# Places of the matmul operands in SBUF, and two MLP rounds written another way, in a one-layer decoder kernel

## The chip, the core and the metric

The kernel runs on one core of one Trainium2 chip. TensorE (PE) multiplies, reading both operands from SBUF and writing to PSUM; VectorE (DVE), ScalarE (ACT) and GpSimd (POOL) do the rest, and SyncE (SP) issues most of the DMAs. The metric is the device time of one execution in microseconds; less is better.

A product on TensorE has a stationary operand of 128x128, brought in by its own instruction (LDWEIGHTS, shown as engine PEld), and a moving operand of 128 rows and up to 512 columns that streams through (MATMUL, engine PE). The profile gives with every stretch the granted clock of TensorE, as a share of full speed.

## What is computed

One layer of a decoder on a sequence of 256 positions of width 2048, in float32:

```python
h = rms_norm(x, norm1_g)
q_a, k_a, v_a, f_a, q_b, k_b, v_b = split(h @ w_in)          # 2048 -> 6 x 1024 + 8
y_a = fox_attention(q_a, k_a, v_a, log_sigmoid(f_a + forget_b))   # 8 heads of 128
y_b = dilated_attention(q_b, k_b, v_b, rel_bias)                  # 8 heads of 128
x = x + concat(rms_norm(y_a, outnorm_a_g), rms_norm(y_b, outnorm_b_g)) @ w_out
h = rms_norm(x, norm2_g)
x = x + square(relu(h @ w_mlp_in)) @ w_mlp_out               # 2048 -> 8192 -> 2048
return rms_norm(x, final_norm_g)
```

## The kernel before

**Split products.** Every large matrix product is made of three: each operand is split into a high part (the value rounded to float32r) and a low part (the rest), and hi x hi, lo x hi and hi x lo are added up in PSUM. Activations are held split, transposed to features x positions: `aT_hi` and `aT_lo` (16 rows of 256 positions on each partition), and `big_hi` and `big_lo`, which serve the attention output (`yT`) first and the hidden layer of the MLP (`hT`) later. A row of 256 float32 is 1024 bytes, so all 16 rows of such a tile begin at the same place in a 256-byte line. An empty tile `ahead` of 8 elements stands before them and shifts that place to element 8 of the line's 64.

**Weights.** They come by DMA from HBM through four buffers `raw` (512 rows x 512 columns each) and are split in steps of 256 rows: ACT copies to `whi` (L178), DVE subtracts and writes `wlo` (L179). Both have four buffers, and each buffer has 64 elements more than it needs, so that a step's data can begin at a chosen place in the line. The places are constants: `LINE, NEAR, HIGH, LOW, GATED = 64, 8, 24, 56, 48`. Where weights are stationary (chunks `q`, `k` and `u`, named in `TURNED`), `whi` begins at element 24 and `wlo` at element 56; where they are the moving operand (`v`, `o`, `d`), both begin at 8; in the one `v` chunk that also holds the forget gates, at 48 and 16, or 56 and 24 for the second row of a step.

**Chunks.** The work is a list of chunks of 512 weight columns: three for each of four head groups (`q`, `v`, `k`), eight for the output projection (`o`), and four MLP rounds (`r` = 0 to 3) of four up chunks (`u`) and four down chunks (`d`). A `u` chunk has 16 feature rows `kt`, and for each 12 products: four blocks of 128 weight columns (stationary) times three terms, with 256 positions moving (`turned_product`, L340). A `d` chunk has for each of 16 `kt` six products: two halves `t` of the positions (stationary) times three terms, with 512 weight columns moving (`product`, L323 to L325). So a `u` half-round has 4 x 16 x 12 = 768 products of 256 columns and a `d` half-round 4 x 16 x 6 = 384 products of 512: 196,608 columns each. The last chunk of all (`last_chunk`) is written in three pieces, the last two with 256 moving columns.

**Order.** The program is written out by hand, engine by engine. Each step's two rows of products are followed by what `at(slot, ...)` hung there: drains of finished accumulators, scores, transposes and values of the attention heads, norms. Weights are split three steps (`LEAD`) ahead of their products and loaded two to three steps ahead of the split. Accumulators have four PSUM banks, two to a chunk.

**Attention scratch.** `scores` writes `neg` (two buffers), which ACT reads for the exponential. `values` squares a head's output into `sqt` (one buffer, L582 and L584), which POOL adds to `sq` (L586).

Of the kernel before, what the change touches and what calls it, by code (L numbers as in the profile page):

```python
# [11 lines left out]
F32 = mybir.dt.float32  # L12
F32R = mybir.dt.float32r
# [6 lines left out]
P = 128  # L20
D_MODEL = 2048
SEQ = 256
TB = SEQ // P
HD = 128
NH = 8
D_GRP = NH * HD
D_FF = 4 * D_MODEL
KT = D_MODEL // P
CW = 512
# [13 lines left out]
LINE, NEAR, HIGH, LOW, GATED = 64, 8, 24, 56, 48  # L43
# [30 lines left out]
def kernel(  # L74
# [18 lines left out]
    nc = tc.nc  # L93
# [5 lines left out]
    lead_in = ctx.enter_context(tc.tile_pool(name="lead_in", bufs=1))  # L99
    one = ctx.enter_context(tc.tile_pool(name="one", bufs=1))  # L100
    two = ctx.enter_context(tc.tile_pool(name="two", bufs=2))
    wraw = ctx.enter_context(tc.tile_pool(name="wraw", bufs=4))
    wsplit = ctx.enter_context(tc.tile_pool(name="wsplit", bufs=LEAD + 1))
    wide = ctx.enter_context(tc.tile_pool(name="wide", bufs=1))
# [6 lines left out]
    chunks = []  # L111
# [25 lines left out]
    raws, splits = {}, {}  # L137
# [15 lines left out]
    def split(i, j0=0, n=2):  # L153
        if i >= len(steps):
            return
        if j0:
            return split_rows(i, j0, n)
        ci, s = steps[i]
        if ci == len(chunks) - 1 and s < 4:
            hi, lo = (a[:, 4 * s:4 * s + 4, :].rearrange("p (k j) s -> p k (j s)", k=2) for a in (aT_hi, aT_lo))  # L160
        else:
            what, cols = chunks[ci][0], chunks[ci][5]
            high, low = (HIGH, LOW) if what in TURNED else (NEAR, NEAR) if cols == CW else (GATED, HIGH - NEAR)
            hi, lo = (
                wsplit.tile([P, 2 * CW + LINE], F32R, name=n)[:, b:b + 2 * cols].rearrange("p (j c) -> p j c", j=2)
                for n, b in (("whi", high), ("wlo", low))
            )
        splits[i] = (hi, lo)
        split_rows(i, j0, n)

    def split_rows(i, j, n):
        ci, s = steps[i]
        hi, lo = (a[:, j:j + n, :] for a in splits[i])
        t = raws[ci, s // 2][:, 2 * (s % 2) + j:2 * (s % 2) + j + n, :chunks[ci][5]]
        cols = t.shape[2]
        step = cols // 2 if i == j == 0 else cols
        for c in range(0, cols, step):
            nc.scalar.activation(hi[:, :, c:c + step], t[:, :, c:c + step], AF.Copy)  # L178
        nc.vector.tensor_tensor(lo, t, hi.bitcast(F32), op=ALU.subtract)  # L179
# [1 line left out]

    xs = one.tile([P, TB, D_MODEL], F32, name="xs")
    grow = one.tile([48, P], F32, name="grow")
    gT = lead_in.tile([P, 96], F32, name="gT")[:, :48]
    ident = one.tile([P, P], F32, name="ident")
    zeros = two.tile([P, CW], F32, name="nat")
    warm = zeros[:, :CW // 2].bitcast(BF16)
# [60 lines left out]
        nc.vector.tensor_copy(gT[:, k0:k1], p[:, k0:k1])  # L248

    wide.tile([P, NEAR], F32, name="ahead")  # L250
    aT_hi = wide.tile([P, KT, SEQ], F32R, name="aT_hi")
    aT_lo = wide.tile([P, KT, SEQ], F32R, name="aT_lo")

    def split_psum(hi, lo, src, scale=None, early=False):

        if early:

            nc.vector.tensor_scalar(hi, src, scale, None, op0=ALU.mult)
            nc.vector.scalar_tensor_tensor(lo, src, scale, hi.bitcast(F32), op0=ALU.mult, op1=ALU.subtract)
        elif scale is None:  # L260
            nc.scalar.activation(hi, src, AF.Copy)  # L261
            nc.vector.tensor_tensor(lo, src, hi.bitcast(F32), op=ALU.subtract)  # L262
        else:
            nc.scalar.activation(hi, src, AF.Copy, scale=scale)
            nc.vector.scalar_tensor_tensor(
                lo, src, scale, hi.bitcast(F32), op0=ALU.mult, op1=ALU.subtract
            )
# [27 lines left out]
    rstd1 = few.tile([P, TB], F32, name="rstd1")  # L295

    def first_squares(t, c):
        unused = yT_hi[:, 2 * (4 * t + c):2 * (4 * t + c) + 2, :].rearrange("p k s -> p (k s)")
        xc = xs[:, t, c * CW:(c + 1) * CW]
        if t == 0:  # L300
            nc.scalar.activation(unused, xc, AF.Square, accum_out=ssq1[:, t, c:c + 1])
        else:
            nc.vector.tensor_tensor_reduce(unused, xc, xc, 1.0, 0.0, ALU.mult, ALU.add, ssq1[:, t, c:c + 1])
# [6 lines left out]
    accs = {}  # L310

    def operands(what, key):
        if what == "o":
            return yT_hi, yT_lo, key[0] * NH
        if what == "d":
            return hT_hi, hT_lo, 0
        return aT_hi, aT_lo, 0

    def product(acc, a, kt, t, w, j, cols, go, end):

        (ah, al, base), (hi, lo) = a, w
        xh, xl = (p[:, base + kt, t * P:(t + 1) * P] for p in (ah, al))
        nc.tensor.matmul(acc, xh, hi[:, j, cols], start=go, stop=False, skip_group_check=True)  # L323
        nc.tensor.matmul(acc, xl, hi[:, j, cols], start=False, stop=False, skip_group_check=True)  # L324
        nc.tensor.matmul(acc, xh, lo[:, j, cols], start=False, stop=end, skip_group_check=True)  # L325

    def turned_product(ci, i, j, kt, kts):


        if kt == 0:  # L330
            accs[ci] = [psum.tile([P, CW], F32, name="acc", bufs=4) for _ in range(2)]
        hi, lo = splits[i]
        terms = ((hi, aT_hi), (hi, aT_lo), (lo, aT_hi))
        order = [(b, n) for b in range(4) for n in range(3)]
        if i == j == 0:
            order.sort(key=lambda bn: bn[1])
        for b, n in order:
            acc = accs[ci][b // 2][:, b % 2 * SEQ:(b % 2 + 1) * SEQ]
            w, a = terms[n]
            nc.tensor.matmul(acc, w[:, j, b * P:(b + 1) * P], a[:, kt, :],  # L340
                             start=kt == 0 and b % 2 == 0 and n == 0, stop=kt == kts - 1 and n == 2,
                             skip_group_check=True)

    def products(i, j):
        ci, s = steps[i]
        what, key, _, _, _, cols, kts = chunks[ci]
        kt = 2 * s + j
        if what in TURNED:
            return turned_product(ci, i, j, kt, kts)
        a = operands(what, key)  # L350
        if cols > CW:
            return gated_products(ci, i, j, kt, kts, a)
        if kt == 0:
            accs[ci] = [psum.tile([P, CW], F32, name="acc", bufs=4) for _ in range(TB)]
        go, end = kt == 0, kt == kts - 1
        for t in range(TB):
            product(accs[ci][t], a, kt, t, splits[i], j, slice(0, CW), go, end)

    def gated_products(ci, i, j, kt, kts, a):

# [87 lines left out]


    qkv = {}  # L450
    yT_hi = wide.tile([P, 2 * NH, SEQ], F32R, name="big_hi")
    yT_lo = wide.tile([P, 2 * NH, SEQ], F32R, name="big_lo")

    def drain_v(g, ci):
# [109 lines left out]
    sq = [one.tile([P, SEQ], F32, name=f"sq{k}") for k in range(2)]  # L564
    seen = [0, 0]

    def values(g, h):
        half, kind = groups[g][3:]
        hd = kind * NH + half * 4 + h
        vh, vl = qkv[g, "v"]  # L570
        p = turned.pop((g, h))
        y = psum.tile([P, 512], F32, name="sc")
        dims = slice(h * P, (h + 1) * P)
        for n, (v, m) in enumerate(((vh, 0), (vh, 1), (vl, 0))):
            nc.tensor.matmul(y[:, :SEQ], v[:, 0, dims], p[:, m, :SEQ], start=n == 0, stop=False,  # L575
                             skip_group_check=True)
        nc.tensor.matmul(y[:, P:3 * P].rearrange("p (n s) -> p n s", n=2), vh[:, 1, dims], p[:, :, SEQ:],  # L577
                         start=False, stop=False, skip_group_check=True)
        nc.tensor.matmul(y[:, P:SEQ], vl[:, 1, dims], p[:, 0, SEQ:], start=False, stop=True, skip_group_check=True)
        first = seen[kind] == 0  # L580
        s = sq[kind] if first else two.tile([P, SEQ], F32, name="sqt", bufs=1)
        nc.scalar.activation(s[:, :P], y[:, SEQ:3 * P], AF.Copy)  # L582
        nc.vector.tensor_tensor(y[:, P:SEQ], y[:, P:SEQ], s[:, :P], op=ALU.add)
        nc.scalar.activation(s, y[:, :SEQ], AF.Square)  # L584
        if not first:
            nc.gpsimd.tensor_tensor(sq[kind], sq[kind], s, op=ALU.add)  # L586
        split_psum(yT_hi[:, hd, :], yT_lo[:, hd, :], y[:, :SEQ], gT[:, 32 + hd:33 + hd])
        seen[kind] += 1
# [29 lines left out]
    hT_hi, hT_lo = yT_hi, yT_lo  # L618

    def drain_u(c, ci):  # L620


        acc = accs.pop(ci)
        for half in range(2):
            h = two.tile([P, CW], F32, name="nat")
            nc.scalar.activation(h, acc[half], AF.Relu)
            nc.vector.tensor_tensor(h, h, h, op=ALU.mult)
            k0 = 4 * c + 2 * half
            split_psum(
                hT_hi[:, k0:k0 + 2, :].rearrange("p k s -> p (k s)"),  # L630
                hT_lo[:, k0:k0 + 2, :].rearrange("p k s -> p (k s)"), h,
            )

    gf = relT.rearrange("p h s -> p (h s)")
    ssq3 = few.tile([P, TB, 5], F32, name="ssq3")
# [79 lines left out]
    for ci, (what, key, *_rest) in enumerate(chunks[:-1]):  # L715
# [9 lines left out]
        elif what in "qk":  # L725
# [3 lines left out]
            if what == "k":  # L729
                kind = groups[key][4]  # L730
                for h in range(4):
                    n = e + 6 + 7 * (h // 2)
# [91 lines left out]
```

## Time and profile before

| what | value |
|---|---|
| median of 2 runs | 1104.89 us (1103.63 to 1106.15) |
| span of the profiled execution | 1214.1 us; its time beyond the span is not on record |
| DVE busy in it | 655.5 us (54%) |
| ACT busy in it | 521.1 us (43%) |
| HBM traffic in it | 205.93 MB read, 171 GB/s over the span |

The profiled execution is 109 us longer than the timed runs, so a duration in the trace is not a duration of a timed run. What the two have in common is the program: the same instructions in the same order. [...]

### The profile page before, as it was taken

Reading aid. Unit: us, or ns where it says so; the run is one execution under the profiler, and the core shown is the slowest. Engines: PE = TensorE matmul, PEld = TensorE weight load, DVE = VectorE, ACT = ScalarE, POOL = GpSimd, SP = SyncE. Lnnn points to the kernel's source line nnn. Section 1 sums busy time; section 2 is a strip of 40 time slices with the busy share of each in tenths; the row PEclk is TensorE's granted clock in tenths of the full one; section 3 lists DMA queues with packets and bytes.
Section 4 is the critical chain, followed back from the end, with each engine's and each line's share of the span. In section 5 each row is a group of like instructions: output and inputs, shape, how many; then the busy total and the mean of one; then the engine's idle time right before and its main releaser. Section 6 shows DMA issues by size and latency. Waiting matters only on the chain.

```text
span 1214.1 us, 17573 instructions
## 1 busy us (share of the span) xinstructions
PE 1201.8 (99%) x7373; PEld 1070.3 (88%) x7373; DVE 655.5 (54%) x837; ACT 521.1 (43%) x687; POOL 27.3 (2%) x42
## 2 busy tenths in 40 slices
PE   9999999999999999999999999999999999999997
PEld 8999898998987799987789997779998779998776
DVE  5666656556566655544544455445545444555563
ACT  5454535445444544443334443334444333444341
POOL 0010200000000000000000000000000000000000
PEclk8888888888888888888888888888888888888887
DMA  8664553544544455555555545555655555545541
GB/s 300 200 209 139 169 178 112 190 160 139 184 153 165 148 174 173 161 187 175 176 175 175 173 170 187 179 170 158 194 183 178 174 173 173 174 147 222 187 139 70
DMA packets 105387, 209.17 MB, mean 172 GB/s; under 512 B 3971, under 2 KB 5084, under 8 KB 105180
## 3 DMA queue, kind: packets, MB, share of 16 engines
q1 hardware_dynamic: 104412, 206.59, 51.6%
q8 instruction: 57, 0.93, 0.3%
q0 software_dynamic: 304, 1.06, 0.2%
q10 hardware_dynamic: 592, 0.40, 0.1%
q14 instruction: 22, 0.18, 0.0%
HBM read 205.93 MB, written 2.11 MB: 171 GB/s over the span
## 4 chain that ended last, share of the span: by engine, by line
PE 99%; DMA 0%; DVE 0%; issue 0%; ACT 0%; POOL 0%; ACTq 0%; DVEq 0%
PE acc L340 48%; PE acc L324 16%; PE acc L323 16%; PE acc L325 16%; PE tr L275 1%; PE sc L575 1%; PE sc L531 0%; PE tr L559 0%; DMA xs<-in_x_dram 0%; PE sc L527 0%; PE sc L577 0%; PE sc L323 0%; PE sc L324 0%; PE sc L325 0%; PE sc L521 0%
## 5 line engine op out<-in xcount | busy, mean ns | idle before, releaser
L179 DVE TENSOR_TENSOR wlo<-raw,whi 128x1024 fp32r<-128x1024 f32 (+2 forms) x382 | 464.0, 1223 | 416.9 <-ACT whi L178 414.8
L178 ACT ACTIVATE whi<-raw 128x1024 fp32r<-128x1024 f32 (+2 forms) x383 | 398.7, 1051 | 475.0 <-PE acc L340 230.1
L340 PE MATMUL acc<-aT_hi,whi 128*128 128x256 f32 x1536 | 450.5, 294 | 0.0
L340 PE MATMUL acc<-aT_hi,wlo 128*128 128x256 f32 x1536 | 446.3, 291 | 0.0
L340 PE MATMUL acc<-aT_lo,whi 128*128 128x256 f32 x1536 | 445.7, 291 | 0.0
L340 PEld LDWEIGHTS acc<-aT_hi,whi 128*128 128x128 f32 x1536 | 306.0, 199 | 1.5 <-ACT p L261 0.7
L340 PEld LDWEIGHTS acc<-aT_lo,whi 128*128 128x128 f32 x1536 | 304.8, 199 | 0.4
L340 PEld LDWEIGHTS acc<-aT_hi,wlo 128*128 128x128 f32 x1536 | 304.9, 199 | 0.0
L324 PE MATMUL acc<-whi,big_lo 128*128 128x512 f32 (+1 forms) x632 | 262.4, 415 | 0.0
L323 PE MATMUL acc<-whi,big_hi 128*128 128x512 f32 (+1 forms) x632 | 262.2, 415 | 0.0
L325 PE MATMUL acc<-wlo,big_hi 128*128 128x512 f32 (+1 forms) x632 | 260.6, 412 | 0.0
L323 PEld LDWEIGHTS acc<-whi,big_hi 128*128 128x128 f32 x632 | 121.6, 192 | 36.1
L325 PEld LDWEIGHTS acc<-wlo,big_hi 128*128 128x128 f32 x632 | 121.6, 192 | 35.9
L324 PEld LDWEIGHTS acc<-whi,big_lo 128*128 128x128 f32 x632 | 121.7, 193 | 34.6
L323 PE MATMUL acc<-whi,aT_hi 128*128 128x512 f32 (+1 forms) x144 | 54.7, 380 | 0.0
L324 PE MATMUL acc<-whi,aT_lo 128*128 128x512 f32 (+1 forms) x144 | 54.1, 376 | 0.0
L325 PE MATMUL acc<-wlo,aT_hi 128*128 128x512 f32 (+1 forms) x144 | 54.1, 376 | 0.0
L262 DVE TENSOR_TENSOR big_lo<-nat,big_hi 128x512 fp32r<-128x512 f32 x32 | 22.2, 692 | 22.4 <-ACT big_hi L261 22.4
L650 DVE SCALAR_TENSOR_TENSOR xs<-acc,rstd2sq,xs 128x512 f32<-128x512 f32 (+1 forms) x33 | 24.2, 734 | 16.2 <-PE acc L325 16.2
L325 PEld LDWEIGHTS acc<-wlo,aT_hi 128*128 128x128 f32 x144 | 27.7, 192 | 5.5
L323 PEld LDWEIGHTS acc<-whi,aT_hi 128*128 128x128 f32 x144 | 27.9, 194 | 5.2
L324 PEld LDWEIGHTS acc<-whi,aT_lo 128*128 128x128 f32 x144 | 27.9, 194 | 5.1
(167 smaller groups left out, 508.4 us busy)
## 6 DMA issues: line engine op xcount, KB each, us to landing
raw<-in_w_mlp_in_dram SPq DMA_DIRECT2D x64, 1024.0 KB, 5.3
raw<-in_w_mlp_out_dram SPq DMA_DIRECT2D x64, 1024.0 KB, 5.1
raw<-in_w_in_dram SPq DMA_DIRECT2D x42, 1024.0 KB, 5.0
raw<-in_w_out_dram SPq DMA_DIRECT2D x16, 1024.0 KB, 5.1
raw<-in_w_in_dram SPq DMA_DIRECT2D x4, 1040.0 KB, 8.1
xs<-in_x_dram SPq DMA_DIRECT2D x3, 512.0 KB, 9.8
raw<-in_w_in_dram SPq DMA_DIRECT2D x2, 512.0 KB, 5.7
big_lo<-rel_d POOLq DMA_DIRECT2D x1, 1024.0 KB, 7.0
```

What stands on the lines that cost most here:

```text
L178: nc.scalar.activation(hi[:, :, c:c + step], t[:, :, c:c + step], AF.Copy)
L179: nc.vector.tensor_tensor(lo, t, hi.bitcast(F32), op=ALU.subtract)
L262: nc.vector.tensor_tensor(lo, src, hi.bitcast(F32), op=ALU.subtract)
L275: nc.tensor.transpose(p[:, j * SEQ + t * P:j * SEQ + (t + 1) * P], xs[:, t, c:c + P], ident)
L323: nc.tensor.matmul(acc, xh, hi[:, j, cols], start=go, stop=False, skip_group_check=True)
L324: nc.tensor.matmul(acc, xl, hi[:, j, cols], start=False, stop=False, skip_group_check=True)
L325: nc.tensor.matmul(acc, xh, lo[:, j, cols], start=False, stop=end, skip_group_check=True)
L340: nc.tensor.matmul(acc, w[:, j, b * P:(b + 1) * P], a[:, kt, :], start=kt == 0 and b % 2 == 0 and n == 0, stop=kt == kts - 1 and n == 2, s ...
L575: nc.tensor.matmul(y[:, :SEQ], v[:, 0, dims], p[:, m, :SEQ], start=n == 0, stop=False, skip_group_check=True)
L650: nc.vector.scalar_tensor_tensor(xs[:, t, cs], acc[:, :cs.stop - cs.start], rstd2sq[:, t:t + 1], xs[:, t, cs], op0=ALU.mult, op1=ALU.add)
```

## The change

**Places.** Rows of `aT_hi`, `aT_lo` and `big_hi` are now 264 elements apart and not 256, so that row `k` begins 8 elements further on in the line than row `k-1`, and every eighth row begins at the same place. `big_lo` keeps its rows. The split weights of `o`, `u` and `d` chunks begin at a place that goes round the line's eight multiples of 8 with step `s` and chunk `ci`, in another manner for `whi` than for `wlo`; those of `q`, `k` and `v` keep theirs. With the rows going round as well, all 8 x 8 pairs of places of the moving and the stationary operand occur. To make room, `gT` loses 48 unused columns, and the squares of `values` use a `neg` buffer where they had `sqt`; so what lies behind `gT` in SBUF moves too.

**Round 1.** Its `u` chunks take the four column blocks one after the other for each term, and its `d` chunks the two halves of the positions for each term, where it was all three terms for each block or half.

**Round 2.** Its `u` chunks take the terms in another order (hi x hi, lo weights x hi, hi x lo activations). Its `d` chunks are computed with 256 moving columns, in twice as many products. Rounds 0 and 3 keep order and width.

```diff
+            if what in "oud":
+                high, low = NEAR * ((s + ci) % 8), NEAR * ((s + 3 * ci + ci // 8 + 1) % 8)
...
-    gT = lead_in.tile([P, 96], F32, name="gT")[:, :48]
+    gT = lead_in.tile([P, 48], F32, name="gT")
...
-    aT_hi = wide.tile([P, KT, SEQ], F32R, name="aT_hi")
-    aT_lo = wide.tile([P, KT, SEQ], F32R, name="aT_lo")
+    ROW = SEQ + NEAR
+    flat = {n: wide.tile([P, KT * ROW], F32R, name=n) for n in ("aT_hi", "aT_lo")}
+    aT_hi, aT_lo = (flat[n].rearrange("p (k s) -> p k s", k=KT)[:, :, :SEQ] for n in ("aT_hi", "aT_lo"))
...
         order = [(b, n) for b in range(4) for n in range(3)]
-        if i == j == 0:
+        if i == j == 0 or chunks[ci][:2] in [("u", (1, c)) for c in range(4)]:
             order.sort(key=lambda bn: bn[1])
+        if chunks[ci][:2] in [("u", (2, c)) for c in range(4)]:
+            order.sort(key=lambda bn: (bn[0], (0, 2, 1)[bn[1]]))
...
+        r = key[0] if what == "d" else 0
+        if r == 1:
+            (ah, al, base), (hi, lo) = a, splits[i]
+            for n, (x, w) in enumerate(((ah, hi), (al, hi), (ah, lo))):
+                for t in range(TB):
+                    nc.tensor.matmul(accs[ci][t], x[:, base + kt, t * P:(t + 1) * P], w[:, j], start=go and n == 0,
+                                     stop=end and n == 2, skip_group_check=True)
+            return
         for t in range(TB):
-            product(accs[ci][t], a, kt, t, splits[i], j, slice(0, CW), go, end)
+            for c in range(0, CW, CW // 2 if r == 2 else CW):
+                cs = slice(c, c + CW // 2 if r == 2 else CW)
+                product(accs[ci][t][:, cs], a, kt, t, splits[i], j, cs, go and c == 0, end)
...
-    yT_hi = wide.tile([P, 2 * NH, SEQ], F32R, name="big_hi")
+    flat["big_hi"] = wide.tile([P, 2 * NH * ROW], F32R, name="big_hi")
+    yT_hi = flat["big_hi"].rearrange("p (k s) -> p k s", k=2 * NH)[:, :, :SEQ]
...
-        s = sq[kind] if first else two.tile([P, SEQ], F32, name="sqt", bufs=1)
+        s = sq[kind] if first else two.tile([P, 3 * P], F32, name="neg")[:, :SEQ]
```

On PE, at the start of the up products of round 1 (`acc` is the accumulator, `aT_hi` and `aT_lo` the moving activations, `whi` and `wlo` the stationary weight blocks), before:

```order
L340 MATMUL acc<-aT_hi,whi 128x256
L340 MATMUL acc<-aT_lo,whi 128x256
L340 MATMUL acc<-aT_hi,wlo 128x256
L340 MATMUL acc<-aT_hi,whi 128x256
L340 MATMUL acc<-aT_lo,whi 128x256
L340 MATMUL acc<-aT_hi,wlo 128x256
```

These are the three terms of the first block and of the second. On PE at the same place now:

```order
L345 MATMUL acc<-aT_hi,whi 128x256 x4
L345 MATMUL acc<-aT_lo,whi 128x256 x4
L345 MATMUL acc<-aT_hi,wlo 128x256 x4
L345 MATMUL acc<-aT_hi,whi 128x256 x4
L345 MATMUL acc<-aT_lo,whi 128x256 x4
L345 MATMUL acc<-aT_hi,wlo 128x256 x4
```

The same twelve products for a feature row now stand in three runs of four, so a block's accumulator is complete later within its twelve.

On PE, at the start of the down products of round 2 (`big_hi` and `big_lo` are the stationary activations, the weights move), before:

```order
L323 MATMUL acc<-whi,big_hi 128x512
L324 MATMUL acc<-whi,big_lo 128x512
L325 MATMUL acc<-wlo,big_hi 128x512
L323 MATMUL acc<-whi,big_hi 128x512
L324 MATMUL acc<-whi,big_lo 128x512
L325 MATMUL acc<-wlo,big_hi 128x512
```

These are the three terms of each half of the positions. On PE at the same place now:

```order
L326 MATMUL acc<-whi,big_hi 128x256
L327 MATMUL acc<-whi,big_lo 128x256
L328 MATMUL acc<-wlo,big_hi 128x256
L326 MATMUL acc<-whi,big_hi 128x256
L327 MATMUL acc<-whi,big_lo 128x256
L328 MATMUL acc<-wlo,big_hi 128x256
L326 MATMUL acc<-whi,big_hi 128x256
L327 MATMUL acc<-whi,big_lo 128x256
L328 MATMUL acc<-wlo,big_hi 128x256
L326 MATMUL acc<-whi,big_hi 128x256
L327 MATMUL acc<-whi,big_lo 128x256
L328 MATMUL acc<-wlo,big_hi 128x256
```

Six products of 512 columns have become twelve of 256, each with a weight load of its own.

On ACT and DVE the instructions and their order stay; only the buffer of the squares differs.

More of the change, by code (lines that the diff above doesn't have):

```diff
@@ L159, in split @@
         if ci == len(chunks) - 1 and s < 4:
-            hi, lo = (a[:, 4 * s:4 * s + 4, :].rearrange("p (k j) s -> p k (j s)", k=2) for a in (aT_hi, aT_lo))
+            hi, lo = (flat[n][:, 1024 * s:1024 * s + 1024].rearrange("p (k c) -> p k c", k=2) for n in ("aT_hi", "aT_lo"))
         else:
@@ L297, in first_squares @@
     def first_squares(t, c):
-        unused = yT_hi[:, 2 * (4 * t + c):2 * (4 * t + c) + 2, :].rearrange("p k s -> p (k s)")
+        unused = flat["big_hi"][:, CW * (4 * t + c):CW * (4 * t + c) + CW]
         xc = xs[:, t, c * CW:(c + 1) * CW]
@@ L628, in drain_u @@
             k0 = 4 * c + 2 * half
[L629 to L632, printed above, removed]
+            split_psum(hT_hi[:, k0:k0 + 2, :], hT_lo[:, k0:k0 + 2, :], h.rearrange("p (k s) -> p k s", k=2))
     gf = relT.rearrange("p h s -> p (h s)")
```

## The prediction

> **What bounds the kernel now.** I read the spans and clocks first, then the busy shares and the chain of work that ended last, then a table of stretches cut at the MLP half-rounds. The view of cores and clocks, and the page:
>
> ```profile
> core 0: 1214.1 us, clock 0.850
> ```
>
> ```profile
> PE 1201.8 (99%) x7373; PEld 1070.3 (88%) x7373; DVE 655.5 (54%) x837; ACT 521.1 (43%) x687; POOL 27.3 (2%) x42
> ...
> PE acc L340 48%; PE acc L324 16%; PE acc L323 16%; PE acc L325 16%; PE tr L275 1%; PE sc L575 1%; PE sc L531 0%; PE tr L559 0%; DMA xs<-in_x_dram 0%; PE sc L527 0%; PE sc L577 0%; PE sc L323 0%; PE sc L324 0%; PE sc L325 0%; PE sc L521 0%
> ```
>
> The chain is TensorE alone, and one core was granted 0.85 of its clock. Whether TensorE was held up by anything but that clock shows in the table of stretches (length, PE busy and count of products, granted clock, DMA share, GB/s):
>
> ```profile
> 0.00:32.30 32.30, 29.94 (x202) 0.89 0.87 305
> 32.30:62.60 30.30, 29.03 (x225) 0.85 0.59 190
> 62.60:434.80 372.20, 372.20 (x2297) 0.85 0.49 163
> 434.80:531.13 96.33, 96.33 (x770) 0.85 0.54 175
> 531.13:627.46 96.33, 96.33 (x387) 0.85 0.52 174
> 627.47:723.80 96.33, 96.33 (x769) 0.85 0.55 176
> 723.80:820.13 96.33, 96.33 (x386) 0.85 0.53 173
> ...
> 1109.12:1205.45 96.33, 96.33 (x432) 0.85 0.42 145
> 1205.45:1214.10 8.65, 0.00 (x1) 0.58 0.32 122
> ```
>
> An up half-round (768 products of 256 columns) and a down half-round (384 of 512) both take 96.33 us: 125.4 ns and 250.9 ns a product. Both are 196,608 columns, so 2,041 columns a us; divided by 0.85 that is 2,401 at full clock. From 62.60 to 1205.45, 1142.85 us, TensorE never stops and pays for columns alone; 71.25 us lie outside (start, first norm, last drains). At full clock the stretch would be 1142.85 x 0.85 = 971.4 us and the execution 971.4 + 71.25 = 1042.7 us.
>
> The timed median is 1104.89 us, 109.2 us below the profiled span. If the 71.25 us stay, TensorE's rate in a timed run is 971.4 / (1104.89 - 71.25) = 0.94 of full. That is an estimate: no record says whether it is a granted clock of 0.94, or a higher one with stalls that the slower clock of the profile hides. Nearly everything that this change can do to the time hangs on this.
>
> **The change part by part**, against the span of 1214.1 us, then carried to the timed runs.
>
> *Half-width down products in round 2.* 384 products become 768 of half the width; the columns stay. Lower bound of the price: zero, and no gain, since no column goes. Three rows speak for zero. The up half-rounds run 768 products, each with its own weight load, in the same 96.33 us. The last half-round already has 96 products of 256 columns with the weights moving, as round 2 gets them, and takes 96.33 us with its 432 products; its last stretch alone:
>
> ```profile
> 1193.40:1205.45 12.05, 12.05 (x97) 0.85 0.23 87
> ```
>
> 96 x 125.4 ns is 12.04 us. And products with fresh stationary operands can follow each other faster still (order of time on PE; start, duration):
>
> ```profile
> 98.06 0.23 PE L521 MATMUL sc<-gate_h,gate_s 128*128 128x128 f32 x1
> 98.11 0.29 PE L525 MATMUL sc<-k,q 128*128 128x128 f32 x1
> 98.24 0.36 PE L527 MATMUL sc<-k,q 128*128 128x256 f32 x1
> ```
>
> Two starts 0.05 us apart, so a load fits well under the 0.113 us that 256 columns take at 0.94 of the clock. Upper bound: loads that no longer overlap. The groups by line have a load at 192 to 199 ns:
>
> ```profile
> L323 PEld LDWEIGHTS acc<-whi,big_hi 128*128 128x128 f32 x632 | 121.6, 192 | 36.1
> L340 PEld LDWEIGHTS acc<-aT_hi,whi 128*128 128x128 f32 x1536 | 306.0, 199 | 1.5 <-ACT p L261 0.7
> ```
>
> 768 x (192 - 125.4) = 51 us. I take 0, the value of the row that does the very same thing.
>
> [...]
>
> *Other orders in rounds 1 and 2.* The products are the same in number and width: 0 on TensorE. What moves is when an accumulator is complete: in the up chunks of round 1 the first one after the 10th of the last twelve products instead of the 6th (4 x 125.4 ns = 0.5 us later), in the down chunks after the 5th of six instead of the 3rd (2 x 250.9 ns = 0.5 us). Waiting behind that are ACT's ReLU and DVE's add to the residual:
>
> ```profile
> ACT nat L626 <- PE acc L340: 21.1, 16, 1.3
> DVE xs L650 <- PE acc L325: 16.2, 18, 5.6
> ```
>
> Their results are due late: the banks are needed again one chunk on, 24 us (a quarter of 96.33), and the hidden rows of the last up chunk in the last quarter of the first down chunk, 18 us on. A weight step's buffers are free with its last product, as before, so splits and loads start as before. Price 0; with the cover gone it would be 0.5 us for each of 8 chunks, 4 us.
>
> *The squares in `neg` and not in `sqt`.* ACT's instruction no longer waits for POOL to empty the one buffer; now DVE's first write of the next group's `neg` waits for POOL's last addition of this one.
>
> ```profile
> ACT sqt L582 <- POOL sq L586: 3.2, 6, 0.6
> ```
>
> What goes is off the chain (TensorE is solid in 62.60:434.80). What comes is an addition done a whole projection of the next group before `scores` needs the buffer. Bounds: -3.2 us if the old wait reached the chain, +3.2 us if the new wait is as long and does. I take 0.
>
> *Places.* Rows further apart and steps that begin elsewhere change no instruction's count or size. For ACT and DVE the price would be longer splits. They are
>
> ```profile
> L179 DVE TENSOR_TENSOR wlo<-raw,whi 128x1024 fp32r<-128x1024 f32 (+2 forms) x382 | 464.0, 1223 | 416.9 <-ACT whi L178 414.8
> L178 ACT ACTIVATE whi<-raw 128x1024 fp32r<-128x1024 f32 (+2 forms) x383 | 398.7, 1051 | 475.0 <-PE acc L340 230.1
> ```
>
> 1.05 + 1.22 us in sequence for a step that TensorE takes 12 x 250.9 ns = 3.0 us over: both would have to grow by a third before it noticed. For TensorE: in the program before, the moving operand's place is 8 and the stationary one's 24 or 56 in up chunks, 8 in down chunks; three of 64 pairs, all at the same 2,041 columns a us. Lower bound 0; the upper one is not in the trace, because at 0.85 of the clock nothing but the clock shows. The nearest measure is the unexplained part of the timed runs, 1104.89 - 1042.7 = 62 us: as much again is the most I can defend. I take 0, since the rows that there are agree to the hundredth of a us.
>
> *Sum.* 0 + 0 + 0 + 0: 1214.1 us for a profiled execution at 0.85, and at the timed runs' rate 1104.89, so 1105 us.
>
> **The rivals.**
>
> *The clock moves down or up.* The program is bound by columns times clock, and the same program shows 0.85 in one execution and about 0.94 in others, so the clock isn't fixed by what the program counts. Other orders make TensorE load a different block at each product where the up chunks loaded `whi` twice running, round 2 loads 384 blocks more, and reads begin at other places; any of these may change what the clock is granted. Against it: within the profile the clock is 0.85 in every stretch, attention, up or down, as different as these are. Half the known distance either way: at 0.895, 971.4 / 0.895 + 71.25 = 1157 us; at 0.985, 1057 us. It decides at 0.92 (1127 us) and 0.96 (1083 us). Chances 0.13 down and 0.20 up. [...]
>
> *Some pairs of places stall TensorE (slower).* If the timed runs have a clock near full and lose 62 us to operands read from unlucky places, constants as particular as 24 and 56 avoid the worst of it, and going round all 64 pairs takes the mean. Its place is every product after 434.80; it decides from 22 us / 6,951 products = 3.2 ns a product, and doubling the 62 us gives 1167 us. Against it: not a sign of it in the trace. Chance 0.18.
>
> *Weight loads bound round 2* (slower, against the three rows above): up to 1104.89 + 51 = 1156 us. Chance 0.03.
>
> *The change does nothing*: places, orders and width all lie beside the bound. That is my forecast.
>
> **How the numbers follow.** Forecast of no change 0.46, with 1095 to 1115 us as its own range; clock up 0.20; clock down 0.13; places 0.18; loads 0.03. A measurement of this kernel tells about 2% from no change, 1083 to 1127 us. So faster 0.20, same 0.46, slower 0.34. The range cuts about half of the clock-up case (below 1065, a clock of 0.98) and half of the place case with a tail of the clock-down case (above 1165): 0.09 + 0.11, so 1065 to 1165 us.
>
> **What would show it.** If I am right, the changed profile has half-rounds that take equal times at one granted clock, the down half-round of round 2 with 768 products among them, and rounds 0 and 3 equal to 1 and 2. Half-rounds of unequal length at one clock mean that places or loads cost; the up half-round of round 0, which has only the places changed, tells which. All half-rounds longer or shorter together, by the granted clock's ratio, means the clock. A gap on PE in the attention stretch would show the `neg` buffer. A timed change with equal granted clocks in both profiles would leave my estimate of 0.94 as the wrong step.

## The result, and the profile after

The changed kernel takes 1137.51 us (median of 2 runs, 1137.10 to 1137.92) where the one before takes 1104.89: a ratio of 1.0297, with a 95% interval of 1.0267 to 1.0328. It is slower by 32.6 us, against a forecast of no change.

The first thing to read in the new profile is the clock. The view of the cores, after the change:

```profile
core 0: 1136.1 us, clock 0.998
```

The profile before the change had 0.850. So the two profiles can't be laid side by side. The kernel before was profiled again, unchanged (experiment 1), and this time was granted the same clock. Its view of the cores:

```profile
core 0: 1104.2 us, clock 0.998
```

With that pair the stretches can be compared. The table of stretches of the changed kernel (start and end, length, PE busy and count of products, granted clock, DMA share, GB/s), cut at the MLP half-rounds; from 404.40 on up and down take turns, round 0 to round 3:

```profile
62.60:404.40 341.80, 341.80 (x2252) 1.00 0.54 173
404.40:496.19 91.79, 91.79 (x777) 1.00 0.59 188
496.19:585.27 89.08, 89.08 (x387) 1.00 0.58 188
585.27:675.79 90.52, 90.52 (x770) 1.00 0.60 189
675.79:764.90 89.11, 89.11 (x387) 1.00 0.58 187
764.90:855.70 90.80, 90.80 (x769) 1.00 0.60 186
855.70:946.46 90.76, 90.76 (x771) 1.00 0.56 185
946.46:1037.40 90.94, 90.94 (x770) 1.00 0.60 187
1037.40:1126.68 89.28, 89.28 (x434) 1.00 0.44 159
1126.68:1136.10 9.42, 0.04 (x1) 0.77 0.30 112
```

The same stretches of the kernel before, in its profile at the full clock:

```profile
62.60:397.60 335.00, 335.00 (x2268) 1.00 0.54 178
397.60:484.75 87.15, 87.15 (x772) 1.00 0.60 195
484.75:571.81 87.06, 87.06 (x386) 1.00 0.59 194
571.81:658.87 87.06, 87.06 (x769) 1.00 0.60 194
658.87:745.94 87.07, 87.07 (x387) 1.00 0.59 193
745.94:833.00 87.06, 87.06 (x770) 1.00 0.61 195
833.00:920.07 87.07, 87.07 (x387) 1.00 0.59 192
920.07:1007.13 87.06, 87.06 (x770) 1.00 0.62 195
1007.13:1094.95 87.82, 87.82 (x434) 1.00 0.46 162
1094.95:1104.20 9.25, 0.03 (x1) 0.74 0.30 114
```

Three things are to be seen. TensorE has no gap in either: busy time equals length in every row but the last. Every half-round has grown, whether its order or width was changed or not: up by 3.5 to 4.6 us, down by 1.5 to 3.7. And it adds up: 6.80 us before the MLP, 4.64 + 2.02 + 3.46 + 2.04 + 3.74 + 3.69 + 3.88 + 1.46 in its half-rounds, 0.17 at the end, together 31.9 us, the difference of the two spans. The loss is paid in small change by all products: 32.6 us over the 6,951 products from 62.60 to 1205.45 of the first profile is 4.7 ns for each, on average.

Even the kernel before does not run at the pace that its clock would allow by an estimate from the first profile: its 2,041 columns a us at a clock of 0.85 scale to 2,401 at a clock of 1. 196,608 columns in 87.06 us are 2,258 a us. 256 columns take 113.4 ns and by that estimate would take 106.6.

### The profile page after: what moved, and what is told of

Its sections match the earlier page's. It is cut to its first block, busy times and chain, and to the rows that moved or that the text cites. A ratio compares the mean times of both kernels' runs of the same rounds, so it can differ in the third digit from the quotient of the medians.

```text
span 1136.1 us, 18333 instructions
## 1 busy us (share of the span) xinstructions
PE 1122.6 (99%) x7757; PEld 1039.3 (91%) x7757; DVE 651.6 (57%) x837; ACT 520.0 (46%) x687; POOL 27.9 (2%) x42
## 4 chain that ended last, share of the span: by engine, by line
PE 98%; DMA 0%; DVE 0%; issue 0%; ACT 0%; POOL 0%; ACTq 0%; DVEq 0%
PE acc L345 48%; PE acc L326 13%; PE acc L327 13%; PE acc L328 13%; PE acc L366 8%; PE tr L278 1%; PE sc L591 1%; PE sc L547 1%; PE tr L575 0%; DMA xs<-in_x_dram 0%; PE sc L543 0%; PE sc L593 0%; PE sc L327 0%; PE sc L326 0%; PE sc L328 0%
## 5 line engine op out<-in xcount | busy, mean ns | idle before, releaser
L345 PE MATMUL acc<-aT_hi,whi 128*128 128x256 f32 x1536 | 401.2, 282 | 0.0
L345 PE MATMUL acc<-aT_hi,wlo 128*128 128x256 f32 x1536 | 399.4, 281 | 0.0
L345 PE MATMUL acc<-aT_lo,whi 128*128 128x256 f32 x1536 | 399.3, 281 | 0.0
L345 PEld LDWEIGHTS acc<-aT_hi,whi 128*128 128x128 f32 x1536 | 275.8, 188 | 1.2 <-issue 0.9
L326 PE MATMUL acc<-whi,big_hi 128*128 128x512 f32 (+1 forms) x632 | 218.7, 346 | 0.0
L328 PE MATMUL acc<-wlo,big_hi 128*128 128x512 f32 (+1 forms) x632 | 218.2, 345 | 0.0
L327 PE MATMUL acc<-whi,big_lo 128*128 128x512 f32 (+1 forms) x632 | 218.2, 345 | 0.0
L366 PE MATMUL acc<-whi,big_lo 128*128 128x512 f32 x128 | 40.1, 394 | 0.0
L366 PE MATMUL acc<-wlo,big_hi 128*128 128x512 f32 x128 | 40.1, 394 | 0.0
L366 PE MATMUL acc<-whi,big_hi 128*128 128x512 f32 x128 | 40.0, 394 | 0.0
```

The source lines that it names most:

```text
L366: nc.tensor.matmul(accs[ci][t], x[:, base + kt, t * P:(t + 1) * P], w[:, j], start=go and n == 0, stop=end and n == 2, skip_group_check=True)
```

## The experiments

All runs compare with the kernel before on the same chip. Three theories were set against each other at first: the places of the operands, the clock, and the orders with the half width.

**1. The kernel before, unchanged.**

> The kernel before, unchanged, for a profile at whatever clock it is granted. Three theories of the 32.6 us that the change costs. PLACES: at the full clock TensorE stalls on operands that begin at unlucky places, and the change takes more of such pairs. Then this run shows a clock near 1.0, a time of about 1105 us, and up and down half-rounds about 2.7 us shorter than the changed kernel's 90.5 to 90.9 and 89.1 us (32.6 us spread over 1142.85 / 96.33 = 11.9 half-rounds): near 88 and 86.4 us. CLOCK: the timed runs of before had a clock of about 0.94 and no stalls; then the clock reads 0.94 and both half-rounds 196,608 / (2400 x 0.94) = 87.1 us. ORDERS: other orders and half width cost it; then at clock 1.0 the half-rounds of rounds 0 and 3 are as long as the changed kernel's, which leaves its 32.6 us to rounds 1 and 2 (in the changed profile rounds 0 to 3 differ by less than 2 us, which speaks against it).

One run: 1106.01 us, clock 0.998; the nine runs of before beside it had a median of 1105.56 us (1103.75 to 1106.92). Both half-rounds take 87.06 us, where PLACES expected about 88 for up and 86.4 for down, and CLOCK 87.1 for both. The 0.94 of the full rate (2,258 of the estimated 2,401 columns a us; the 2,400 of the expectations is that estimate, rounded) is there, as CLOCK had it, but at a granted clock of 0.998: it is what TensorE makes of this kernel's products, and not the clock. CLOCK is out.

**2. Only the rows go round.**

```diff
+    ROW = SEQ + NEAR
+    flat = {n: wide.tile([P, KT * ROW], F32R, name=n) for n in ("aT_hi", "aT_lo")}
+    aT_hi, aT_lo = (flat[n].rearrange("p (k s) -> p k s", k=KT)[:, :, :SEQ] for n in ("aT_hi", "aT_lo"))
...
+    flat["big_hi"] = wide.tile([P, 2 * NH * ROW], F32R, name="big_hi")
...
-        s = sq[kind] if first else two.tile([P, SEQ], F32, name="sqt", bufs=1)
+        s = sq[kind] if first else two.tile([P, 3 * P], F32, name="neg")[:, :SEQ]
```

> Before with the rows of aT_hi, aT_lo and big_hi 264 elements apart (the squares in neg to make room; everything else begins where it did). PLACES: rows alone bring the moving operand of the up chunks and the stationary one of the down chunks to all eight places, against weights at one place: up to the whole loss, 1120 to 1137 us. CLOCK and ORDERS: no change, 1105 us.

1134.43 us, ratio 1.0263 (1.0247 to 1.0278): nearly the whole loss. Its stretches, the down half-round of round 0 and the up half-round of round 1:

```profile
496.00:585.10 89.10, 89.10 (x387) 1.00 0.58 188
585.10:675.53 90.43, 90.43 (x770) 1.00 0.59 188
```

**3. Only the weights go round.**

```diff
+            if what in "oud":
+                high, low = NEAR * ((s + ci) % 8), NEAR * ((s + 3 * ci + ci // 8 + 1) % 8)
```

> Before with the places of split weights of o, u and d chunks going round as in the change, rows 256 apart. PLACES: eight of eight pairs against one place of the activations, in some 70% of the products: 1115 to 1130 us. CLOCK and ORDERS: 1105 us.

1129.02 us, ratio 1.0215 (1.0199 to 1.0231). The same two stretches:

```profile
489.78:578.84 89.06, 89.06 (x387) 1.00 0.58 189
578.84:669.65 90.81, 90.81 (x769) 1.00 0.58 187
```

Either part alone brings the half-rounds to the length that they have with both. So the two don't add up: 28.9 us and 23.5 us alone, 32.6 us with everything. Where one part has already broken the pace, the other adds little.

**4. Only the orders and the half width.**

> Before with the orders of round 1 and 2 and the half-width down products of round 2 alone, places as before. ORDERS: the whole loss, 1137 us. PLACES: at most the 1.7 us by which the changed kernel's half-width down half-round (90.8 us) is longer than its others (89.1): 1106 to 1107 us. CLOCK: 1137 us if the other orders are what moves the clock, with a granted clock below that of before.

1109.17 us, ratio 1.0036 (1.0024 to 1.0049). Up and down half-round of round 1, then of round 2:

```profile
569.99:657.10 87.11, 87.11 (x769) 1.00 0.61 196
657.10:744.17 87.07, 87.07 (x387) 1.00 0.58 191
744.17:831.21 87.04, 87.04 (x769) 1.00 0.61 193
831.21:923.37 92.16, 92.16 (x770) 1.00 0.56 184
```

Three of the four are at 87.0 to 87.1 us: at these places the orders cost nothing. The half-width half-round takes 92.16 us, 5.1 us more, three times what PLACES allowed it (1.7 us, from a profile in which the wide ones were already slow). ORDERS is out as the cause of the loss, and the expectation of PLACES was too small. With places settled as the cause, the next runs asked what about them counts.

**5. The weights follow the rows.** Rows of `aT_hi` and `aT_lo` go round as in run 2, and the weights of `q`, `k` and `u` go with them.

```diff
+            row = cols
+            if what in TURNED:
+                high, low, row = (high + 2 * NEAR * s) % LINE, (low + 2 * NEAR * s) % LINE, cols + NEAR
...
-                wsplit.tile([P, 2 * CW + LINE], F32R, name=n)[:, b:b + 2 * cols].rearrange("p (j c) -> p j c", j=2)
-                for n, b in (("whi", high), ("wlo", low))
+                wsplit.tile([P, 2 * CW + LINE + NEAR], F32R, name=n)[:, b:b + 2 * row].rearrange("p (j c) -> p j c", j=2)[:, :, :cols]
+                for n, b in (("whi", (high - NEAR * (-i % 4)) % LINE), ("wlo", (low - 4 * NEAR - NEAR * (-i % 4)) % LINE))
```

> Before with the rows of aT_hi and aT_lo 264 elements apart, and the split weights of q, k and u chunks following them: both rows of a step begin 8 elements further on as well, so that every product of these chunks keeps the distance between moving and stationary place that it had before (16 elements behind for whi, 16 ahead of wlo, in a line of 64), at all eight places of the line. big_hi keeps its rows, o and d chunks are as before. DISTANCE (the distance of the two places decides, wherever they are): up half-rounds 87.1 us, 1105.6 us in all. CHANGE (any move of a place from one row to the next breaks the even pace): up half-rounds near the 90.4 us of rows alone, +13.5 us for four of them and some 4 us in q and k: about 1122 us.

1123.59 us, ratio 1.0170 (1.0155 to 1.0185). The down half-round of round 0, which is untouched, and the up half-round of round 1:

```profile
492.27:579.33 87.06, 87.06 (x387) 1.00 0.59 192
579.33:669.39 90.06, 90.06 (x770) 1.00 0.59 189
```

DISTANCE falls and CHANGE holds. The starts of the products show how; a product's own duration (0.28 us in runs 1, 5 and 6) overlaps those of the next ones, which start 0.11 to 0.12 us apart. Worked out from the traces, the mean time in ns from each start to the next, over the twelve products of a feature row in the up and `q`/`k` chunks (the first row of a chunk, and rows with other products between, are left out):

```
run 1, all rows at element 8                     113 113 113 113 113 113 113 113 113 113 113 113
run 5, weights follow rows, row at element 16    118 118 117 118 122 118 115 120 118 113 113 115
run 5, weights follow rows, row at element 40    118 118 118 118 122 118 115 120 118 113 113 115
run 2, weights stay, row at element 8            118 118 117 117 122 118 115 120 118 113 113 113
run 2, weights stay, row at element 16           116 118 123 114 118 117 123 116 116 120 123 117
run 2, weights stay, row at element 40           113 113 114 114 114 114 114 114 114 114 114 114
```

In run 5, where both operands begin 8 elements further on with each row, nine products go by before the pace of 113 ns is there again; three products later comes the next row, and the same again, wherever in the line the row stands. Run 2 shows that a move need not cost that: rows at element 40 keep the pace almost from their first product, though the row before begins elsewhere; rows at element 8 find it after nine; at the other six places the pace does not return within the twelve. Rows eight apart, which begin at the same place of different lines, take the same time in run 2 to within 6 ns in some 1,400; rows four apart, at elements 8 and 40, differ in nearly every column of the table. So the place counts in run 2 by its position in the 256-byte line.

**6. One place for all, and none moves.**

```diff
-            high, low = (HIGH, LOW) if what in TURNED else (NEAR, NEAR) if cols == CW else (GATED, HIGH - NEAR)
+            high, low = (NEAR, NEAR) if what in TURNED else (NEAR, NEAR) if cols == CW else (GATED, HIGH - NEAR)
```

> Before with the stationary weights of q, k and u chunks at element 8 and not at 24 and 56: moving and stationary operand begin at one place, and none ever moves. DISTANCE: the price that half-width products at distance 0 had (92.16 against 87.07 us for 768 products, +6.6 ns each): up half-rounds near 92.2 us, +20 us for four and +10 us for the 1536 products of q and k, about 1136 us. CHANGE: nothing moves, 1105.6 us and 87.1 us.

1134.30 us, ratio 1.0270 (1.0253 to 1.0288). The up half-round of round 1:

```profile
584.73:676.89 92.16, 92.16 (x770) 1.00 0.58 185
```

Here each product takes 120 ns, all of them alike: 3,057 of 3,068 distances from start to start in the up half-rounds are 120 ns, whatever the other engines and the DMA do meanwhile. Their work does not show in the pace here, though no run tests that alone. The number is DISTANCE's, and CHANGE as the only cause falls: there are steady arrangements that never find the pace. Down products of 512 columns, level in the same way, keep it (87.06 us).

**7. Everything 16 elements further on.**

```diff
-    gT = lead_in.tile([P, 96], F32, name="gT")[:, :48]
+    gT = lead_in.tile([P, 48], F32, name="gT")
```

> Before with gT 48 columns narrower, so that all operands begin 16 elements further on in the line (192 bytes lower in SBUF), their distances unchanged. DISTANCE and CHANGE: 1105.6 us, half-rounds 87.1 us. PLACE (single places in the line are good or bad by themselves): another time; the full loss would be about 1130 us.

1104.82 us, ratio 0.9999 (0.9990 to 1.0009): nothing. This part of the change is free, and PLACE is out as far as one shift, by 16 elements, can show.

**8 and 9. Half-width down products at other places.** The down products of round 2 alone have half the width, with orders as before; `whi` and `wlo` stand at 24 and 56, then both at 24.

```diff
+            if what == "d" and chunks[ci][1][0] == 2:
+                high, low = HIGH, LOW
...
+                high, low = HIGH, HIGH
```

> Before with half-width down products in round 2 alone, and their split weights at elements 24 and 56, so that the moving weights stand 16 elements ahead of the stationary activations or 16 behind, and not level with them. DISTANCE: the half-round falls from 92.2 to 87.1 us, 1105.6 us. WIDTH (twice as many products with moving weights cost 5 us by themselves): 92.2 us and about 1110.5 us.

1107.73 us, ratio 1.0032 (1.0019 to 1.0046). The half-width half-round with 24 and 56:

```profile
832.77:923.22 90.45, 90.45 (x770) 1.00 0.57 186
```

Neither theory's number: the distances are those that up products keep pace with, but now it is the moving operand that goes between two places.

> Before with half-width down products in round 2, whi and wlo both at element 24: the moving operand is 16 elements ahead of the stationary one in every product and never changes its place. PACE (a steady distance sets a steady pace, and a moving operand that begins elsewhere than the one before it breaks the pace for up to ten products): the 90.4 us of the run with 24 and 56 came from the moving operand going to and fro, so now 87.1 us and about 1104.5 us. WIDTH (twice as many products with the weights moving cost by themselves): still 90 us or more.

1104.27 us, ratio 0.9997 (0.9988 to 1.0007). The same half-round with both at 24:

```profile
831.40:918.44 87.04, 87.04 (x771) 1.00 0.59 193
```

WIDTH is out: 768 narrow products cost no more (87.04 us) than 384 wide ones (87.07 us in run 1) where the moving operand keeps one suitable place. The 5.1 us of run 4 were a matter of places too.

**10. The weights follow the rows, `whi` and `wlo` exchanged.** The edit against run 5:

```diff
-                high, low, row = (high + 2 * NEAR * s) % LINE, (low + 2 * NEAR * s) % LINE, cols + NEAR
+                high, low, row = (low + 2 * NEAR * s) % LINE, (high + 2 * NEAR * s) % LINE, cols + NEAR
```

> As the run in which the weights follow the rows, but with the places of whi and wlo exchanged (the moving row 16 elements ahead of whi and 16 behind wlo). In the rows-alone run, rows at element 40, which stand so to the weights, kept the pace of 113 to 114 ns from their first or second product, where rows at element 8 took nine products to find it. If which side the stationary operand lies on decides how soon the pace is found again: up half-rounds 87.1 to 87.5 us, about 1105 us. If every change of the moving place costs the same: 90.06 us as in the other run, about 1122 us.

1124.61 us, ratio 1.0171 (1.0154 to 1.0188); the up half-round of round 1:

```profile
581.78:672.06 90.28, 90.28 (x770) 1.00 0.59 189
```

The second expectation: over a row, a change costs about the same on this side. Why rows at element 40 recovered at once in run 2 is not explained by the side.

**11 and 12. Other steady places.** `whi` and `wlo` at one element for a whole round: 24, 40, 56 and then as before; 16, 32, 48, 0.

```diff
+            if what in "ud" and chunks[ci][1][0] < 3:
+                high = low = (24, 40, 56)[chunks[ci][1][0]]
...
+            if what in "ud":
+                high = low = (16, 32, 48, 0)[chunks[ci][1][0]]
```

> Before with whi and wlo of round 0, 1 and 2 at element 24, 40 and 56, in up and in down chunks; round 3 as before. No place changes within a half-round, so each shows the steady pace of one distance (16, 32, 48 of 64). PACE: up with 24 or with 56 alone 87.1 us, since both distances occur at that pace in before; for down chunks with 512 columns the level distance 0 is the only known one at 87.1 us, others may be as slow as 92 us. CHANGE alone (a constant distance of any kind is as good as another): down half-rounds all 87.1 us.

One run, 1121.07 us. Down round 0 (element 24), then up and down of round 1 (40), of round 2 (56), and up of round 3 (24 and 56, as before):

```profile
486.54:574.46 87.92, 87.92 (x387) 1.00 0.58 190
574.46:665.59 91.13, 91.13 (x769) 1.00 0.58 187
665.59:754.81 89.22, 89.22 (x387) 1.00 0.58 187
754.81:845.26 90.45, 90.45 (x770) 1.00 0.59 188
845.26:934.86 89.60, 89.60 (x387) 1.00 0.56 187
934.86:1021.95 87.09, 87.09 (x770) 1.00 0.61 194
```

A miss for PACE: up products with 56 alone take 90.45 us, though that distance occurs in every row of before at its pace. With 24 alone it is no better: the up half-round of round 0 takes 91.33 us, from 395.21 on, against 87.96 us in run 1, from 396.79 on. In these up chunks the pace was there only with the two places together. CHANGE alone misses as well: none of these three down half-rounds reaches 87.1.

Nor does a steady distance set the pace, even at one width. In run 9 the moving operand (24) stands 16 elements ahead of the stationary one (8); here in round 2 the moving operand (8) stands 16 ahead of the stationary one (56), counted round the line. Both have 768 products of 256 columns and nothing moves, yet the one half-round takes 87.04 us and the other 90.45. What else differs between them (which operand is the activations, and in what order blocks are taken) was not tested.

> The same with elements 16, 32, 48 and 0 in rounds 0 to 3: the distances 8, 24, 40 and 56 of 64. PACE: half-rounds between 87.1 and 92.2 us, each steady from product to product, none below 87.1. If some distance let TensorE take its columns at the full 2,400 a us, its half-round would be 81.9 us; no row so far is below 113.3 ns for 256 columns, so I expect none.

One run, 1129.08 us. Down round 0 (16), up and down of round 1 (32), of round 2 (48), up of round 3 (0):

```profile
486.62:576.22 89.60, 89.60 (x386) 1.00 0.57 187
576.22:666.33 90.11, 90.11 (x769) 1.00 0.58 188
666.33:755.94 89.61, 89.61 (x387) 1.00 0.57 187
755.94:848.09 92.15, 92.15 (x769) 1.00 0.58 185
848.09:938.05 89.96, 89.96 (x386) 1.00 0.58 186
938.05:1028.50 90.45, 90.45 (x769) 1.00 0.59 188
```

As expected, between 87.1 and 92.2 us, and none below; but not each is steady from product to product: at 48, up products take 116 to 125 ns in a pattern that repeats (worked out from the trace). No run found an arrangement faster than that of before.

## Why the forecast was wrong

The measured time lies in the range (1065 to 1165 us), and one of the rivals describes what happened; the likeliest case, no change, was wrong. That the range holds the time is in part luck: the cases of another clock, which did not occur, made much of its width, and the rival that did had its own price above it.

*The step that failed* is the price of the places: "I take 0, since the rows that there are agree to the hundredth of a us." Those rows agree at a clock of 0.85, where TensorE takes 2,041 columns a us, less than the 2,258 that it takes at 0.998 in the best arrangement; 125.4 ns for 256 columns is also more than the 120.0 ns of the worst steady up half-round in the runs, 92.16 us. The prediction said itself that "at 0.85 of the clock nothing but the clock shows", and then counted such rows as evidence against the rival. They were no evidence. One such row was even a bad case in the kernel before: the last 96 products, the stretch 1193.40:1205.45 of the prediction. At 0.85 they take 12.05 us, the time of their columns; at a clock of 0.998 (run 1):

```profile
1083.44:1094.95 11.51, 11.51 (x97) 1.00 0.24 91
```

That is 120 ns for each and not 113.4, so the slower clock hid a cost that was there. (The changed places themselves were not profiled at 0.85.) The price of the places is measured by runs 2 and 3: 28.9 us for the rows alone and 23.5 us for the weights alone.

*The estimate of 0.94* was right as a rate (2,258 of the estimated 2,401). Of its two readings the second holds: "a higher one with stalls that the slower clock of the profile hides". The prediction had said that a changed time at equal clocks would leave this estimate as the wrong step; it is not, since stalls at an equal clock were one of its readings. At the full clock of 1 the prediction's own sum gave 1042.7 us, 62 us below the timed runs; by that estimate those 62 us are what this kernel pays even at the places of before. The loss of the change, 32.6 us, is half of that. The rival's price, another 62 us and 1167 us, was twice too high; its point of decision, 3.2 ns a product, was passed with 4.7 ns. It placed the loss after 434.80, but its 6,951 products are those from 62.60 on; after 434.80 there are 4,657. The loss does begin at 62.60, with 6.80 us before the MLP.

*The rival's mechanism* was only partly right. It had 64 pairs of places, good and bad. Run 5 shows that a pair that is good when it stays (87.06 us) is bad when it moves along the line (90.06 us), and run 11 that a place good in turn with another is bad alone (90.45 us with 56, 91.33 with 24). Run 9 against run 11 shows that pairs at one distance and width can differ (87.04 and 90.45 us). What counts is the sequence of places, and something more that no run here isolates.

*Half width at 0* was wrong in size: +5.1 us at the places of before (run 4); in the changed kernel 90.76 against 89.08 us in round 0, +1.7 us. The row taken as its double is the one above, and it hid that price; at the full clock the last half-round takes 87.82 us and not 87.06. Weight loads do not bound it, as the prediction had it: with 768 products and a suitable place it takes 87.04 us (run 9).

*The orders at 0* were right (87.04 to 87.11 us in run 4, at the places of before). *The `neg` buffer at 0* is borne out as far as PE goes: no gap from 62.60 to 404.40. *The clock* as a rival did not occur: 0.998 before and after, and 0.997 or 0.998 in the profile of every run, so no run shows orders, loads or places moving it. Whether the clock of 0.850 in the first profile has a cause in that execution, or in the chip that it ran on, no run here tells.

*What stays open* is what in the machine sets the pace. The trace has starts and durations of products and weight loads, and nothing of how operands are fetched. Shown is that operand places decide, for products equal in count, size and order (runs 2, 3 and 6). Why they do was not shown. No rule found here foretells the pace from the places: DISTANCE, CHANGE and PACE each failed in some run. Rows set apart by a whole 256-byte line, which would move nothing in the line, were not tried either.

## What to carry over

Read the granted clock before anything else: a profile at a lower clock than the timed runs' can hide a limit that lies between the two, and rows that agree there say nothing about it. Here the last 96 products took 12.05 us at 0.85, no more than their columns, and at 0.998 120 ns each where others took 113.4. Where TensorE is the bound and never idle, divide its columns by the time; a rate below the granted one, here an estimated 0.94 at a clock of 0.998, is a cost that no gap shows, and where operands begin in SBUF is then worth a try. Start with the moving operand of successive products at one place in the 256-byte line and rows a whole number of lines apart (up half-rounds of 87.06 us in run 1, and of 90.43 in run 2 with rows 264 elements apart). That alone is not enough (run 6, 92.16 us), so try the places of the weights in whole rounds, for each product width by itself.

## What the hardware did that was not expected

With places that stay the same from row to row, 256 moving columns take between 113.4 and 120.0 ns at a clock of 0.998. The whole of that difference lies between the up half-rounds of run 1 and run 6 (87.06 and 92.16 us), which differ only in where the weights begin, by 64 and 192 bytes; with places as steady, a half-round of 512-column products varies between 87.06 and 89.96 us. No run here shows another engine slowing TensorE's products (in run 6, 3,057 of 3,068 distances are the same 120 ns); but its pace does hang on where its own two operands begin, 87.06 against 92.16 us.

Where both operands move on together with each row (run 5), the pace is lost for about nine products, 1 us, and then found again without any gap; after other moves it is kept, or not found within twelve products (run 2). The best pace seen is 6% above the columns' own time as estimated from the first profile (2,258 columns a us against 2,401), and is the same for 768 products of 256 columns and for 384 of 512 (87.06 us), so here it's paid for columns and not for products. With a weight load for each product, 256 columns take 113.4 ns and 512 take 226.7 ns at best: twice the columns take twice the time, and no fixed part for each product shows.
